# A hybrid decoder trunk on one core: the residual's scale and shift on GpSimd and the router's column sums on VectorE moved to later places, and fourteen instead of two clock-keeping products ahead of the second layer

## The chip, the cores and the metric

The kernel runs on one core of a Trainium2 chip. The metric is the device time of one execution in microseconds. TensorE (PE in the rows) multiplies matrices into PSUM; VectorE (DVE), ScalarE (ACT) and GpSimd (POOL) do the elementwise work; SyncE (SP) issues the transfers. Each engine runs its own instructions strictly in the order of its queue.

## The reference, cut to what matters

Two layers over 256 tokens of width 1024. Each has a token mixer with three branches (latent attention "mla", gated delta rule "dn", HGRN2 "hg"), gated, merged and projected, and then a mixture of experts, each followed by a layer norm of the residual:

```python
h = layer_norm(x, ln_in_g, ln_in_b)
for l in range(DEPTH):
    proj = h @ w_in[l]
    ...
    mixed = (g_a * y_a + g_b * y_b + g_c * y_c) @ w_out[l]
    h = layer_norm(DEEPNORM_ALPHA * h + mixed, ln1_g[l], ln1_b[l])
    moe_out = hier_moe(h, router_group_w[l], router_group_b[l], ...)
    h = layer_norm(DEEPNORM_ALPHA * h + moe_out, ln2_g[l], ln2_b[l])
```

The router inside `hier_moe` multiplies `h` by a 1024 x 36 matrix (4 groups, 32 experts) and adds a bias.

## The kernel before, in words

The input projection's weights come in chunks of up to 1 MB, in a fixed order (`ORDER`), through four buffers. ScalarE rounds a chunk to a high part (L249) and VectorE, for four chunks GpSimd, takes the rest as a low part (L250, "the split"); TensorE adds three products for each pair (L261 to L263, "dense products" here). The branches' small steps lie between dense products on TensorE's queue, so that dense products fill waits as long as there are some ahead of the waiting step.

A layer starts with the norm's statistics on VectorE. A diagonal matrix of the inverse deviations is built from them (tile `sg`, L621), and sixteen products with it turn the residual (L395; each stands in the rows as two). ScalarE and VectorE then write `hTh` and `hTl`, which the dense products read. The norm's true output, which the residual needs only when the mixer's result is added in `project_out`, is made apart: ScalarE scales the tile `res` (L642), GpSimd multiplies it by the norm's weight and adds its bias, 128 x 1024 at a time for two blocks of tokens (L376, L377). The weight and bias lie in two tiles named `o`.

The attention of four heads runs as: query and key products (L1227), query times its rotary table (L1229), scores (L1248), masked maximum on VectorE (L1255), exponentials on ScalarE (L1257), division (L1259, L1261), turning of the weights (L1264) and the product with the values (L1270).

`router_sums` prepares the router's constants. GpSimd multiplies the router's matrix by the norm's weight and bias (L567), VectorE sums over eight slices (L570, 128 x 576 to 128 x 72), adds a bias (L571), TensorE adds over partitions with a matrix of ones, and VectorE copies the result (L574). It is called last in the mixer, but a scheduler sets the order of each engine's queue by what is ready, and `issue_after` puts an instruction behind a named one. So L567 and L570 stood early, at the attention's scores.

Behind the experts of the first layer stands a branch for overflowing experts, which is not taken here. `warm(n)` issues n products of 128 x 128 by 128 x 512 ones in bf16 whose result nobody reads: ten ahead of the branch, two behind it.

Of the kernel before, what the change touches and what calls it, by code (L numbers as in the profile page):

```python
# [15 lines left out]
OP = mybir.AluOpType  # L16
AX = mybir.AxisListType
# [90 lines left out]
class Trunk:  # L108
# [451 lines left out]
        q.dma_start(gb[:, 1], A["ln1_b"][l].rearrange("(p k) -> p k", k=8))  # L560
        self.gb1 = gb[:, 0], gb[:, 1]

    def router_sums(self):

        nc, rw, p = self.nc, self.rw, self.hp
        for i in range(2):
            nc.gpsimd.tensor_tensor(rw[:, :, 36 * i:36 * i + 36], rw[:, :, 36:72],  # L567
                                    self.gbr[i][:, :, None].to_broadcast([128, KT, 36]), op=OP.mult)
        self.rsum = p.tile([128, 72], F32, name="rsum", tag="rsum")
        nc.vector.tensor_reduce(self.rsum, rw.rearrange("p k c -> p c k"), axis=AX.X, op=OP.add)  # L570
        nc.vector.tensor_add(self.rsum[0:1, 36:72], self.rsum[0:1, 36:72], self.rb)  # L571
        ps = self.ps()
        nc.tensor.matmul(ps[:, 0:72], self.ones, self.rsum, start=True, stop=True)
        nc.vector.tensor_copy(self.rsum, ps[:, 0:72])  # L574
# [16 lines left out]
    def layer(self, l):  # L591
        tc, side = self.tc, dict(side="right")
        with ExitStack() as cl, ExitStack() as cr:
            self.ctx_l = cl
            self.sp = cr.enter_context(tc.tile_pool(name=f"split{l}", bufs=1, **side))
            self.gp = cr.enter_context(tc.tile_pool(name=f"merge{l}", bufs=1, **side))
            xp = cr.enter_context(ExitStack())
            hp = xp.enter_context(tc.tile_pool(name=f"x{l}", bufs=1, **side))
            oc = cr.enter_context(ExitStack())
            self.op = oc.enter_context(tc.tile_pool(name=f"o{l}", bufs=1, **side))  # L600
            with tc.tile_pool(name=f"mix{l}", bufs=1) as mp:
                self.mp = mp
                self.open_small(mp, 256)
                if l == 0:
                    rope, src = self.buf("d8", [128, 8, T]), self.A["positions"]
                    self.nc.sync.dma_start(rope[:, 0].bitcast(I32),
                                           bass.AP(tensor=src.tensor, offset=src.offset, ap=[[0, 128], [1, T]]))
                    self.issue(self.wp)
                self.mixer_consts(l, mp)
                if l == 0:  # L610
                    for _ in range(self.NBUF - 2):
                        self.issue(self.wp)
                    self.vrows = self.small_weights(l)
                self.mla_weights(l)
                gb = [x.rearrange("p h t -> p (h t)") for x in self.o4(F32)]
                for x, n in zip(gb, "gb"):
                    self.bcast_row(x, self.A["ln_in_" + n] if l == 0 else self.A["ln2_" + n][l - 1], D)
                self.hT = [hp.tile([128, KT, T], F32R, name=n, tag=n) for n in ("hTh", "hTl")]
                diag = self.gp.tile([128, 4, 128], F32, name="sg", tag="sg", bufs=self.NB["sg"])
                for t in range(TB):  # L620
                    self.nc.vector.tensor_scalar(diag[:, t], self.ident, self.hrs[:, t], None, op0=OP.mult)  # L621
                self.transposed(self.h, self.hT, self.gb0, tmp=lambda: self.buf("d2", [128, 2, T]), scale=diag)
                if l == 0:
                    with tc.issue_after(self.latest(self.nc.tensor)):
                        self.warm(8)
                    with tc.issue_after(self.last_lo.ins):
                        self.rope_tables(rope)
                self.router_weights(l)
                self.mix = self.gp.tile([128, TB, D], F32, name="mix")

                self.pq = self.ps("pm")
                self.chunk_cm(self.pq, l, "cq")
                seq = "dn_decay mla h0 dn_keys dn_inverse dn_queries h1 " \
                      "dn_values hg_forget hg_project hg_local dn_scan hg_scan"
                for n in seq.split():
                    f, a = (self.mla_heads, (int(n[1]),)) if n in ("h0", "h1") else (getattr(self, n), ())
                    self.bank = "pb" if n[:2] == "dn" else "pm"
                    f(l, mp, *a)
                    if f == self.mla:
                        with tc.issue_after(self.last_exp.ins):  # L640
                            for t in range(TB):
                                self.nc.scalar.activation(self.h[:, t], self.h[:, t], AF.Copy, scale=self.hrs[:, t])  # L642
                        with tc.issue_after(self.pool_last.ins):
                            self.scaled(self.h, gb[:1], gb[1:], self.nc.gpsimd)
                        if l == 0:
                            self.nc.gpsimd.tensor_copy(self.bits[:, 1], self.cst("ustrict"))
                        self.dump(f"h2_{l - 1}", self.h.rearrange("p t d -> p (t d)"))
                self.bank = None
                self.merge_branch(l, "a")
                self.gates(l, mp)  # L650
                self.branch_gate(l, mp, "dn", self.dn_o)
                self.branch_gate(l, mp, "hg", self.hg_o)
                self.router_sums()
            self.pw = self.open_prefetch(f"prefetch{l}", self.NPRE)
            self.merge_branch(l, "b")
            def between():

                self.mixS = [hp.tile([128, 8, T], F32R, name=n, tag=n) for n in ("hTh", "hTl")]
                self.mix_turned(0)

            self.merge_branch(l, "c", between)

            oc.close()
            self.open_prefetch(f"more{l}a", 2)

            def free():
                xp.close()
                self.open_prefetch(f"more{l}b", 2)

            self.project_out(l, free)  # L670
            cr.close()
            self.open_prefetch(f"more{l}c", 1)
            with tc.tile_pool(name=f"h1_{l}", bufs=1, **side) as xp, tc.tile_pool(name=f"moe{l}", bufs=1, **side) as ep, \
                    ExitStack() as yc:
                self.moe(l, xp, ep, yc, self.h)
# [5 lines left out]
    def dn_decay(self, l, mp):  # L681
# [57 lines left out]
        nc.vector.tensor_tensor(E, psg.rearrange("p (a i) -> p a i", i=C), c8(gc[:, 0:8]), op=OP.subtract)  # L739
        nc.vector.tensor_tensor(E, E, b8(mincl), op=OP.mult)  # L740
        self.last_exp = nc.scalar.activation(E, E, AF.Exp)
        self.pool_last = nc.gpsimd.tensor_tensor(E, E, b8(mincl), op=OP.mult)
        self.E = E
        ex = self.small([128, 32])
        nc.scalar.activation(ex[:, 0:8], gc[:, 0:8], AF.Exp)
# [378 lines left out]
    def branch_gate(self, l, mp, n, o):  # L1124
        nc = self.nc
        ov = o.rearrange("p t h e -> p (t h) e")
        gv = self.gate[n].rearrange("p t h e -> p (t h) e")
        ss, rs = self.small([128, 8]), self.small([128, 8])
        for i in range(8):
            junk = self.gp.tile([128, 128], F32, name="sg", tag="sg", bufs=self.NB["sg"])  # L1130
            nc.scalar.activation(junk, ov[:, i], AF.Square, accum_out=ss[:, i:i + 1])
        if n == "dn":
            nc.vector.scalar_tensor_tensor(ss, ss, 1.0 / 128, self.dn_eps, op0=OP.mult, op1=OP.add)
        else:
            nc.vector.tensor_scalar(ss, ss, 1.0 / 128, 4 * EPS, op0=OP.mult, op1=OP.add)
        self.rsqrt(rs, ss, self.small([128, 8]))
        for i in range(8):
            nc.vector.scalar_tensor_tensor(ov[:, i], ov[:, i], rs[:, i:i + 1], gv[:, i], op0=OP.mult, op1=OP.mult)
        oT = self.o4()
        for i in range(0, 4, 2):  # L1140
            ps = self.ps()
            for ii in range(2):
                for t in range(TB):
                    nc.tensor.transpose(ps[:, 256 * ii + 128 * t:256 * ii + 128 * t + 128], o[:, t, i + ii], self.ident)
            hi, lo = (x[:, i:i + 2].rearrange("p h t -> p (h t)") for x in oT)
            nc.scalar.activation(hi, ps, AF.Copy, scale=self.on[n])
            nc.vector.scalar_tensor_tensor(lo, ps, self.on[n], hi.bitcast(F32), op0=OP.mult, op1=OP.subtract)
        self.oT[n] = oT
        self.dump_oT(l, n)
# [382 lines left out]
    def moe(self, l, xp, ep, yc, h1):  # L1532
# [200 lines left out]
            self.in_turn(self.warm, 10)  # L1733
        self.overflow(l, ep, rv, past, cmb, xc, total, st)
        if l + 1 < DEPTH:
            self.warm(2)
            self.centred(acc, total, st)
            self.open_banks(f"mix_banks{l}", self.MIX_BANKS, None)
            return
# [53 lines left out]
```

## Time and profile before

| | us |
|---|---|
| median of three runs (1183.57 to 1183.85) | 1183.82 |
| the profiled execution's own time | 1185.7 |
| its span, first instruction to last | 1183.8 |
| TensorE busy in it | 1069.7 (90%) |
| VectorE, ScalarE, GpSimd busy | 593.6, 451.4, 178.7 |
| mean granted clock of TensorE | 0.955 |

A busy share is a mean over stages with different limits. The first layer runs from 0 to about 592 us, the second from there to the end, and each has its mixer first and its experts behind. The granted clock is 1.00 at 2.4 GHz and 0.50 at 1.2 GHz.

### The profile page before, as it was taken

What the parts mean: (1) busy time and instruction counts of PE and PEld (TensorE: products, weight loads), DVE (VectorE), ACT (ScalarE), POOL (GpSimd) and SP (SyncE); (2) the same over time, 40 slices, a digit from 0 to 9 for tenths busy, and PEclk for the clock granted to TensorE, in tenths of its full rate; (3) what the DMA queues carried; (4) which work ended last, traced back from release to release, by engine and by line L of the source; (5) the groups of instructions that cost most, each with busy time, mean ns of one, the idle gap of its engine ahead of it and who ended that gap; (6) DMA issues with size and microseconds to landing.
All of it is one profiled execution on the core that took longest, in us unless ns stands there. A gap on an engine that the chain in (4) does not pass through costs nothing. (4 is left out here: it accounts for less than half of the span.)

```text
span 1183.8 us, 21451 instructions
## 1 busy us (share of the span) xinstructions
PE 1069.7 (90%) x8884; PEld 778.4 (66%) x8884; DVE 593.6 (50%) x1281; ACT 451.4 (38%) x812; POOL 178.7 (15%) x160
## 2 busy tenths in 40 slices
PE   7799998999999999777789999989999999987775
PEld 5688985777777655444377889667777775644442
DVE  7477848466456433111167876574755553321114
ACT  5564553354444222100057545435544442211111
POOL 2410016101120400000024110250012103000001
PEclk9899998999999999888889999989999999988887
DMA  7531341257986799999982314213499669999995
GB/s 231 183 109 37 109 143 37 84 167 292 419 352 225 315 426 425 427 426 427 400 246 74 108 38 143 77 68 126 159 397 424 244 233 417 425 425 426 427 427 207
DMA packets 104706, 305.58 MB, mean 258 GB/s; under 512 B 20962, under 2 KB 48028, under 8 KB 79516
## 3 DMA queue, kind: packets, MB, share of 16 engines
q1 hardware_dynamic: 104604, 304.15, 66.9%
q8 instruction: 72, 1.18, 0.4%
q14 instruction: 30, 0.25, 0.1%
HBM read 303.08 MB, written 1.05 MB: 257 GB/s over the span
## 5 line engine op out<-in xcount | busy, mean ns | idle before, releaser
L250 DVE TENSOR_TENSOR wl<-w,wh 128x1024 fp32r<-128x1024 f32 x150 | 185.6, 1238 | 160.0 <-ACT wh L249 157.3
L249 ACT CAST wh<-w 128x1024 fp32r<-128x1024 f32 x158 | 165.7, 1049 | 199.5 <-PE ps_po L263 68.7
L1620 PE MATMUL ps_pa<-w,xg 128*32 128x256 f32 x2304 | 173.2, 431 | 57.3 <-DMA w<-in_exp_w_up_dram 28.1
L1620 PEld LDWEIGHTS ps_pa<-w,xg 128*32 128x32 f32 x2304 | 84.6, 123 | 140.2 <-DMA w<-in_exp_w_up_dram 37.2
L1632 DVE SCALAR_TENSOR_TENSOR hm<-ps_pa,ws,hm 128x256 f32<-128x256 f32 x18 | 8.7, 484 | 200.7 <-ACT hm L1631 200.5
L1631 ACT ACTIVATE hm<-ps_pa 128x256 f32<-128x256 f32 x18 | 6.9, 385 | 218.7 <-PE ps_pa L1620 218.7
L1653 PE MATMUL ps_pm<-w,hmT 128*32 128x512 f32 x576 | 72.4, 595 | 1.3 <-issue 1.3
L261 PE MATMUL ps_pa<-wh,hTh 128*128 128x512 f32 x176 | 71.4, 405 | 2.0 <-ACT hTh L254 0.7
L261 PE MATMUL ps_po<-wh,hTh 128*128 128x512 f32 x176 | 71.3, 405 | 2.0 <-ACT hTh L254 0.7
L262 PE MATMUL ps_pa<-wl,hTh 128*128 128x512 f32 x176 | 71.1, 404 | 0.9 <-POOL wl L250 0.6
L262 PE MATMUL ps_po<-wl,hTh 128*128 128x512 f32 x176 | 71.0, 404 | 0.9 <-POOL wl L250 0.6
L263 PE MATMUL ps_po<-wh,hTl 128*128 128x512 f32 x176 | 70.9, 403 | 0.2 <-DVE hTl L255 0.2
L263 PE MATMUL ps_pa<-wh,hTl 128*128 128x512 f32 x176 | 70.6, 401 | 0.2 <-DVE hTl L255 0.2
L1570 PEld LDWEIGHTS ps_pm<-P,h1c 128*128 128x128 f32 x576 | 66.8, 192 | 2.2 <-ACT res L1368 1.0
L1570 PE MATMUL ps_pm<-P,h1c 128*128 128x128 f32 x576 | 67.3, 275 | 0.1
L1579 ACT ACTIVATE xg<-ps_pm,gb 128x128 f32<-128x128 f32 x72 | 33.0, 458 | 74.6 <-DVE xg L1577 74.6
L1592 POOL TENSOR_TENSOR Pw<-P,small 128x128 f32<-128x128 f32 x32 | 12.4, 407 | 306.0 <-PE ps_pm L1599 229.5
L1297 POOL TENSOR_TENSOR mix<-mix,sg 128x512 f32<-128x512 f32 x16 | 28.3, 1794 | 153.0 <-DVE sg L1295 153.0
L1577 DVE TENSOR_SCALAR xg<-ps_pm,gb 128x128 f32<-128x128 f32 x72 | 29.4, 408 | 41.1 <-PE ps_pm L1570 32.1
L263 PE MATMUL ps_po<-hTh,wl 128*128 128x256 f32 (+1 forms) x168 | 48.9, 291 | 0.9 <-DVE wl L250 0.5
L261 PE MATMUL ps_pa<-hTh,wh 128*128 128x256 f32 (+1 forms) x168 | 49.5, 295 | 0.0
L263 PE MATMUL ps_pa<-hTh,wl 128*128 128x256 f32 (+1 forms) x168 | 49.0, 292 | 0.5 <-DVE wl L250 0.5
(460 smaller groups left out, 2206.5 us busy)
## 6 DMA issues: line engine op xcount, KB each, us to landing
w<-in_exp_w_gate_dram SPq DMA_DIRECT2D x66, 1024.0 KB
w<-in_exp_w_up_dram SPq DMA_DIRECT2D x66, 1024.0 KB
w<-in_exp_w_down_dram SPq DMA_DIRECT2D x64, 1024.0 KB
w<-in_w_in_dram SPq DMA_DIRECT2D x58, 1024.0 KB
w<-in_w_out_dram SPq DMA_DIRECT2D x8, 1024.0 KB
w<-in_w_br_a_dram SPq DMA_DIRECT2D x4, 1024.0 KB
w<-in_w_br_b_dram SPq DMA_DIRECT2D x4, 1024.0 KB
w<-in_w_br_c_dram SPq DMA_DIRECT2D x4, 1024.0 KB
```

What stands on the lines that cost most here:

```text
L249: nc.scalar.copy(v(hi), raw)
L250: engine.tensor_tensor(v(lo), raw, v(hi).bitcast(F32), op=OP.subtract)
L261: mm(ps, a[0], b[0], start=start, stop=False, skip_group_check=True)
L262: mm(ps, a[0], b[1], start=False, stop=False, skip_group_check=True)
L263: mm(ps, a[1], b[0], start=False, stop=stop, skip_group_check=True)
L1297: nc.gpsimd.tensor_tensor(mv, mv, sg[t], op=OP.add)
L1570: nc.tensor.matmul(ps[:, 128 * k:128 * k + 128], xc[:, t, 4 * h + k], Ps[q][:, t], start=(t == 0), stop=(t == 1))
L1577: nc.vector.tensor_scalar(xg[:, k], o, g, b, op0=OP.mult, op1=OP.add)
L1579: nc.scalar.activation(xg[:, k], o, AF.Identity, scale=g, bias=b)
L1592: self.pool_last = nc.gpsimd.tensor_tensor(e(Pw[:, t]), e(P[:, t]), w, op=OP.mult)
L1620: nc.tensor.matmul(pg[32 * e:32 * e + 32, FF * n:FF * n + FF], xgs[q][k // 4][:, k % 4, 32 * e:32 * e + 32], w[:, FF * k:FF * k + FF], sta ...
L1653: nc.tensor.matmul(ps[c][32 * e:32 * e + 32], hmT[:, i, 32 * e:32 * e + 32], ws[e][:, D * i + 512 * c:D * i + 512 * c + 512], start=(i == ...
```

## The change

Three edits. The four GpSimd instructions that finish the residual are called behind the mixer's scans, and behind whatever stands last on GpSimd's queue there. The router's sum on VectorE is put behind the last instruction of the hg branch's gate (`last_gate`). Behind the overflow branch fourteen clock-keeping products stand instead of two.

```diff
-    def router_sums(self):
+    def router_sums(self, after):
...
-        nc.vector.tensor_reduce(self.rsum, rw.rearrange("p k c -> p c k"), axis=AX.X, op=OP.add)
+        with self.tc.issue_after(after):
+            nc.vector.tensor_reduce(self.rsum, rw.rearrange("p k c -> p c k"), axis=AX.X, op=OP.add)
...
-                        with tc.issue_after(self.pool_last.ins):
-                            self.scaled(self.h, gb[:1], gb[1:], self.nc.gpsimd)
-                        if l == 0:
-                            self.nc.gpsimd.tensor_copy(self.bits[:, 1], self.cst("ustrict"))
...
+                with self.tc.issue_after(self.latest(self.nc.gpsimd)):
+                    self.scaled(self.h, gb[:1], gb[1:], self.nc.gpsimd)
+                    if l == 0:
+                        self.nc.gpsimd.tensor_copy(self.bits[:, 1], self.cst("ustrict"))
...
-                self.router_sums()
+                self.router_sums(self.last_gate.ins)
...
         for i in range(8):
-            nc.vector.scalar_tensor_tensor(ov[:, i], ov[:, i], rs[:, i:i + 1], gv[:, i], op0=OP.mult, op1=OP.mult)
+            self.last_gate = nc.vector.scalar_tensor_tensor(ov[:, i], ov[:, i], rs[:, i:i + 1], gv[:, i], op0=OP.mult,
+                                                            op1=OP.mult)
...
         if l + 1 < DEPTH:
-            self.warm(2)
+            self.warm(14)
             self.centred(acc, total, st)
```

Line numbers of the changed kernel are up to three higher. GpSimd's queue in the first layer, around the residual (`res`), the router's matrix (`rw`) and the delta rule's first tile (`d`), before:

```order
L736 TENSOR_TENSOR d_423<-small,mconst 128x512
L742 TENSOR_TENSOR d_424<-d_424,mconst 128x512
L376 TENSOR_TENSOR res<-res,o_193 128x1024
L377 TENSOR_TENSOR res<-res,o_194 128x1024
L376 TENSOR_TENSOR res<-res,o_193 128x1024
L567 TENSOR_TENSOR rw<-rw,vcols 128x8x36
L377 TENSOR_TENSOR res<-res,o_194 128x1024
L567 TENSOR_TENSOR rw<-rw,vcols 128x8x36
L847 MEMSET d_816 128x1024
```

The same place now:

```order
L738 TENSOR_TENSOR d_423<-small,mconst 128x512
L744 TENSOR_TENSOR d_424<-d_424,mconst 128x512
L567 TENSOR_TENSOR rw<-rw,vcols 128x8x36 x2
L849 MEMSET d_811 128x1024
L875 TENSOR_TENSOR d_809<-d_775,mconst 128x256 x2
```

The four `res` instructions have left it; they stand behind the last GpSimd instruction of the hg scan (L1110 before) and ahead of the next split on GpSimd. VectorE's queue in the second layer, ahead of the attention's scores, before:

```order
L739 TENSOR_TENSOR d_5652<-ps_pb,small 128x512
L255 TENSOR_TENSOR egl<-small,egh 128x8
L570 TENSOR_REDUCE rsum<-rw 128x72
L740 TENSOR_TENSOR d_5652<-d_5652,mconst 128x512
L1197 SCALAR_TENSOR_TENSOR a_5700<-ps_pm,vcols,a_5701 128x256 x2
L1199 SCALAR_TENSOR_TENSOR a_5700<-ps_pm,vcols,a_5701 128x256
L571 TENSOR_TENSOR rsum<-rsum,rb 1x36
L1229 TENSOR_TENSOR a_5733<-ps_pm,qtab 128x512
```

And now:

```order
L741 TENSOR_TENSOR d_5664<-ps_pb,small 128x512
L255 TENSOR_TENSOR egl<-small,egh 128x8
L742 TENSOR_TENSOR d_5664<-d_5664,mconst 128x512
L1200 SCALAR_TENSOR_TENSOR a_5712<-ps_pm,vcols,a_5713 128x256 x2
L1202 SCALAR_TENSOR_TENSOR a_5712<-ps_pm,vcols,a_5713 128x256
L1232 TENSOR_TENSOR a_5741<-ps_pm,qtab 128x512
```

The sum and its bias are gone from there. In the first layer the sum stood directly ahead of the first masked maximum (L1255), and is gone from there too. VectorE's queue in the first layer behind the hg branch's gate (the instruction on `a` x6 is the gate's last six of eight), before:

```order
L1138 SCALAR_TENSOR_TENSOR a_2231<-a_2231,small,a_2588 128x128 x6
L574 COPY rsum<-ps_pb 128x72
L250 TENSOR_TENSOR wl<-w,wh 128x1024
L1147 SCALAR_TENSOR_TENSOR o_2752<-ps_pb,vcols,o_2751 128x512
L1147 SCALAR_TENSOR_TENSOR o_2752<-ps_pm,vcols,o_2751 128x512
```

And now:

```order
L1140 SCALAR_TENSOR_TENSOR a_2226<-a_2226,small,a_2588 128x128 x6
L571 TENSOR_REDUCE rsum<-rw 128x72
L250 TENSOR_TENSOR wl<-w,wh 128x1024
L1150 SCALAR_TENSOR_TENSOR o_2752<-ps_pb,vcols,o_2751 128x512
L1150 SCALAR_TENSOR_TENSOR o_2752<-ps_pm,vcols,o_2751 128x512
L572 TENSOR_TENSOR rsum<-rsum,rb 1x36
```

The sum now stands ahead of a split that TensorE's next dense products read, and the small copy has gone behind the split after it. On ScalarE the second layer's second rounding (L249) now stands ahead of the first step that reads the turned residual instead of behind it. On SyncE, one load of an expert's weights stands ahead of a load of a projection chunk that it followed before.

## Rows read from the trace of the kernel before

**Rows 1.** Waits of TensorE over the span, the longest: us in total, times, longest us.

```profile
PE ps_pa L1620 <- DMA w<-in_exp_w_up_dram: 28.1, 17, 1.9
```

**Rows 2.** Timeline of TensorE, first layer: start us, duration us, instruction, [idle before].

```profile
46.79 0.60 PE L1248 MATMUL ps_pm<-a,a 128*128 128x128 f32 x4
...
56.62 1.08 PE L1264 MATMUL ps_pm<-const,a 128*128 128x128 f32 x4 [7.44 <-DVE a L1261]
...
60.95 0.58 PE L263 MATMUL ps_po<-hTh,wl 128*128 128x256 f32 x1
```

**Rows 3.** Timeline of VectorE, first layer.

```profile
52.87 1.18 DVE L570 TENSOR_REDUCE rsum<-rw 128x72 f32<-128x576 f32 x1 [6.60 <-POOL rw L567]
53.97 0.28 DVE L1255 CUSTOM_DVE_ANT_0 a<-ps_pm,mconst 128x128 f32<-128x128 f32 x1
...
56.19 0.87 DVE L1261 TENSOR_SCALAR a<-a,mla_st 128x128 f32<-128x128 f32 x4
57.53 1.23 DVE L250 TENSOR_TENSOR wl<-w,wh 128x1024 fp32r<-128x1024 f32 x1 [0.47 <-ACT wh L249]
```

**Rows 4.** Timeline of GpSimd, first layer, first of the residual's four.

```profile
42.12 2.37 POOL L376 TENSOR_TENSOR res<-res,o 128x1024 f32<-128x1024 f32 x1 [0.67 <-ACT res L642]
```

**Rows 5.** Busy time by window, first layer; behind the engines: granted clock, DMA share, GB/s.

```profile
55.00:60.00 5.00, 3.34 (x15) 2.41 (x16) 3.51 (x9) 4.73 (x12) 0.00 (x0) 0.50 0.00 0
```

**Rows 6.** Timeline of TensorE, the second layer's start.

```profile
592.00 2.33 PE L365 MATMUL ps_pa<-bits 128*128 128x512 bf16 x10
594.63 0.59 PE L365 MATMUL ps_pa<-bits 128*128 128x512 bf16 x2 [0.30 <-DVE ln_v L333]
598.00 3.76 PE L395 MATMUL ps_pm<-sg,res 128*128 128x128 f32 x16 [2.77 <-DVE sg L621]
601.54 3.08 PE L395 MATMUL ps_pb<-sg,res 128*128 128x128 f32 x16
...
606.79 0.39 PE L262 MATMUL ps_pm<-hTl,wh 128*128 128x256 f32 x1 [1.22 <-DVE hTl L255]
```

**Rows 7.** Busy time by window, the second layer's start.

```profile
598.00:602.00 4.00, 4.00 (x19) 4.00 (x20) 0.75 (x2) 2.70 (x4) 1.19 (x1) 0.50 1.01 239
```

**Rows 8.** Timeline of TensorE, the first layer's start.

```profile
11.09 1.95 PE L395 MATMUL ps_pm<-sg,res 128*128 128x128 f32 x16
```

**Rows 9.** Waits of TensorE from 592 to 640 us.

```profile
PE ps_pm L1264 <- DVE a L1261: 1.7, 1, 1.7
...
PE ps_pm L1203 <- ACT d L741: 0.7, 1, 0.7
```

**Rows 10.** Timeline of VectorE, second layer, around the scores.

```profile
630.59 1.78 DVE L250 TENSOR_TENSOR wl<-w,wh 128x1024 fp32r<-128x1024 f32 x1 [0.39 <-ACT wh L249]
...
636.15 2.34 DVE L1261 TENSOR_SCALAR a<-a,mla_st 128x128 f32<-128x128 f32 x4
```

**Rows 11.** Timeline of VectorE, first layer, behind the gate.

```profile
277.47 0.22 DVE L574 COPY rsum<-ps_pb 128x72 f32<-128x72 f32 x1
277.61 1.21 DVE L250 TENSOR_TENSOR wl<-w,wh 128x1024 fp32r<-128x1024 f32 x1
```

**Rows 12.** Timeline of TensorE, first layer, behind the gate.

```profile
278.88 0.50 PE L262 MATMUL ps_pa<-wl,hTh 128*128 128x512 f32 x1 [0.35 <-DVE wl L250]
```

**Rows 13.** Timelines of GpSimd, VectorE and TensorE, first layer, behind the hg scan.

```profile
214.74 1.05 POOL L1110 TENSOR_TENSOR a<-a,small 128x512 f32<-128x512 f32 x1 [0.80 <-DVE a L1111]
...
223.91 1.23 DVE L250 TENSOR_TENSOR wl<-w,wh 128x1024 fp32r<-128x1024 f32 x1 [5.17 <-ACT wh L249]
...
226.18 0.40 PE L262 MATMUL ps_pa<-wl,o 128*128 128x512 f32 x1
```

**Rows 14.** Busy time by window, ahead of the first layer's experts.

```profile
385.00:395.00 10.00, 10.00 (x157) 7.04 (x155) 5.11 (x35) 3.63 (x10) 0.88 (x2) 1.00 0.35 130
```

**Rows 15.** Timelines of SyncE's queue and ScalarE: a load, and a later rounding of its chunk.

```profile
270.03 8.48 SPq L180 DMA_DIRECT2D w<-in_w_in_dram  x2
...
296.10 1.05 ACT L249 CAST wh<-w 128x1024 fp32r<-128x1024 f32 x1 [2.15 <-PE ps_po L263]
```

More of the change, by code (lines that the diff above doesn't have):

```diff
@@ L642, in layer @@
                                 self.nc.scalar.activation(self.h[:, t], self.h[:, t], AF.Copy, scale=self.hrs[:, t])
-                        with tc.issue_after(self.pool_last.ins):
-                            self.scaled(self.h, gb[:1], gb[1:], self.nc.gpsimd)
-                        if l == 0:
-                            self.nc.gpsimd.tensor_copy(self.bits[:, 1], self.cst("ustrict"))
-                        self.dump(f"h2_{l - 1}", self.h.rearrange("p t d -> p (t d)"))
-                self.bank = None
+                self.bank = None
+                with tc.issue_after(self.latest(self.nc.gpsimd)):
+                    self.scaled(self.h, gb[:1], gb[1:], self.nc.gpsimd)
+                    if l == 0:
+                        self.nc.gpsimd.tensor_copy(self.bits[:, 1], self.cst("ustrict"))
+                self.dump(f"h2_{l - 1}", self.h.rearrange("p t d -> p (t d)"))
                 self.merge_branch(l, "a")
@@ L741, in dn_decay @@
         self.last_exp = nc.scalar.activation(E, E, AF.Exp)
-        self.pool_last = nc.gpsimd.tensor_tensor(E, E, b8(mincl), op=OP.mult)
+        nc.gpsimd.tensor_tensor(E, E, b8(mincl), op=OP.mult)
         self.E = E
```

## The prediction

> **What bounds the kernel now.** I read the page's busy times first (in the table above): TensorE works 90% of the span, so a gain has to come out of its idle time, or out of work that it does at the lower clock. Then its waits, longest first. The longest in total belongs to the experts, where TensorE waits for weights, 28.1 us for one of three kinds, never over 1.9 us at a time [rows 1]; the change doesn't touch that. The longest single waits inside the mixers lie at the edits: ahead of L1264 in the first layer, and ahead of L395 at the second layer's start. The timelines around these two show who is late, and the windows show what clock TensorE had behind them.
>
> In the first layer the scores end at 46.79 + 0.60 = 47.39 [rows 2], but the masked maximum that reads them starts at 53.97 [rows 3]. Ahead of it on VectorE's queue stands the router's sum, which waited 6.60 us for GpSimd's product L567, and GpSimd was busy with the residual's four instructions of 2.37 us from 42.12 [rows 3, 4]. So a sum that only the router needs holds up the attention, and TensorE, out of dense products, stands still for 7.44 us [rows 2]. Behind it the clock is 0.50 [rows 5].
>
> **The change, part by part.** I sum in microseconds; minus is a gain.
>
> *A, the first layer's scores.* With the sum gone, the maximum starts at 47.4 instead of 53.97. From there to L1264 took 56.62 - 53.97 = 2.65 [rows 2, 3]; ScalarE and VectorE lie idle otherwise, and I keep it. L1264 then starts at 50.1, which is 6.5 earlier. TensorE waits under 1 us instead of 7.44 (its dense products ran out at 56.62 - 7.44 = 49.18), and I expect the clock to stay. Before, the stretch from L1264 to the dense product at 60.95, 4.33 us, ran at 0.50 [rows 2, 5]. At full clock its products would take half, but it also holds two trips through ScalarE and VectorE, among them the split that this very product reads, 57.53 + 1.23 = 58.76 [rows 3]. That split comes 6.5 earlier too, so the product could start some 2 us sooner beyond the shift; I take 1.3. A = -6.5 - 1.3 = -7.8, bounds -6.5 (no clock gain) and -8.5.
>
> *B, the second layer's start.* Ten clock-keeping products took 2.33, 0.23 each at 1.00 [rows 6]. Twelve more are 2.8, and the idle time that they fall into is 2.77 [rows 6], so fourteen end about when the diagonal is there: cost 0, at most 0.4. What they buy: TensorE had been idle for 2.77 us, and the thirty-two turning products behind it ran at 0.50 [rows 7], in 3.76 + 3.08 = 6.84 [rows 6]. In the first layer, with busy products right ahead, sixteen of the same took 1.95 [rows 8], so 3.9 for both halves: -2.9. Behind them the dense products then stopped for `hTl` for 1.22 [rows 6]. That chain on VectorE and ScalarE hangs on the turning products and starts earlier; a rounding that stood in the middle of it on ScalarE's queue (about 1 us) now stands ahead of it in idle time. I take 1.0 of the 1.22. B = -3.9, bounds -2.5 and -4.3.
>
> *C, the second layer's scores.* Here GpSimd did its part in time, and the sum ran at once, but directly ahead of the steps that the attention's products needed; TensorE waited 0.7 there. Later it waited 1.7 for the division [rows 9], which took 2.34 instead of 0.87 [rows 3, 10] while GpSimd still worked on the residual. Both causes leave: C = -0.7 - 1.6 = -2.3, bounds -1.7 and -2.6.
>
> *D, the sum at its new place.* It takes 1.18 [rows 3], and the copy of 0.22 that it displaces goes behind the next split. The split behind it ended at 277.61 + 1.21 = 278.82, and TensorE already waited 0.35 for it [rows 11, 12]. So nothing covers the difference: 1.18 - 0.22 = 1.0 us in each layer. D = +2.0, bounds 0 (if TensorE finds products that don't need the split) and 2.8 (if the copy, late now, still costs as much elsewhere).
>
> *E, the residual at its new place.* GpSimd is free from 214.74 + 1.05 = 215.8 [rows 13], and four times 2.37 end at 225.3. Nobody reads the residual until the projection. GpSimd's next instruction is a split for the dn gate, behind the whole merge of the first branch, so I count nothing for its queue. VectorE's work in that stretch is little, but the split at 223.91 falls into it, and TensorE reads its result at 226.18 [rows 13]. The same kind of split met GpSimd at 630.59 and took 1.78 instead of 1.23 [rows 3, 10]; so it would end at 225.7, in time. The most that a row shows, the division's 1.47, gives 226.6, 0.4 late. I take 0, bounds 0 and 0.8 for both layers.
>
> The rows show VectorE slowed beside GpSimd by very different amounts. The Trainium skill, "SBUF — State Buffer", section "SBUF: two separate sides", has a rule for that: the two engines share a pair of ports as an exclusive lock, and whoever comes second waits for the whole instruction of the other. The division agrees with it: it starts at 636.15 and ends only at 638.49. By that rule the split at 223.91 waits for the last of the four to end at 225.3, ends at 226.5, and TensorE loses 0.3 in each layer: the sum would be 0.6 worse.
>
> *Whether the gain reaches the end.* Ahead of the first layer's experts the transfers move at 0.35 of the engines' share [rows 14]: the buffers are full, and loading goes on when TensorE frees them. So the experts' stage, where transfers set the pace, starts earlier by what the mixer gained, and the same holds in the second layer.
>
> Sum: -7.8 - 3.9 - 2.3 + 2.0 + 0 = -12.0. The profiled execution took 1185.7, so 1173.7 for one with a profile. The runs' median, 1183.82, is 1.9 less and equals the span; from it the sum gives **1171.8**.
>
> **The rivals.**
> 1. *The clock is not kept.* If the fourteen don't hold it, or it falls behind the shorter wait of A, what is left is 6.5 + 1.0 + 2.3 - 2.0 = 7.8: 1176.0. Speaking for it: TensorE still waits near 1 us in A, and the clock has fallen after waits. Against: in the first layer's start the same pattern of products kept 1.95 per sixteen [rows 8].
> 2. *The sums cost nothing more and the dense stretch profits in full.* The far ends of A to C and the near end of D: -8.5 - 4.3 - 2.6 + 0 = -15.4, so 1168.4. It needs slack behind the gate, and none shows [rows 12].
> 3. *The transfers take it back.* If loading of experts were the limit from the mixer on, all gains ahead of it would be lost: no change. The share of 0.35 speaks against it [rows 14].
> 4. *Slower: the load that was passed.* On SyncE's queue an expert's load now stands ahead of a projection chunk's load, and it waits for a buffer that the split behind the moved sum frees. Before, the chunk's load was issued at about 278 (270.03 + 8.48), and its rounding started at 296.10, kept by TensorE and not by the transfer [rows 15]. So there are 18 us less one transfer of slack. Each microsecond beyond that stops TensorE in both layers; over 6 us in each eat the 12.0, that is a load that comes some 24 us late. The split is done about 280, which makes that unlikely.
>
> **How the numbers follow.** The forecast with its bounds gets 0.70, rival 1 0.12, rival 2 0.12, rival 3 0.03, rival 4 0.03. The forecast's own bounds, not all at one end, give 1170 to 1175; rivals 1 and 2 widen the range to 1168 to 1177.5. A measurement of this kernel can tell about 0.2%, 2.4 us, from no change. Forecast and rivals 1 and 2 are faster by more, rival 3 is the same, rival 4 slower: 0.94, 0.03, 0.03.
>
> **What would show it.** In the profile after: the masked maximum right behind the scores near 47.4, L1264's counterpart near 50, and a granted clock of 1.00 from 50 to 60 (A). Fourteen products that end near 598 without a fall of the clock, both halves of the turning in about 4 us, and no wait for `hTl` (B). No wait of 0.7 or 1.7 at the second layer's scores (C). TensorE's wait behind the gate grown from 0.35 to about 1.3 in each layer (D). No wait for the split near 226 less the shift (E). The prediction is wrong if the sum behind the gate holds TensorE for longer, if the fourteen products run past the diagonal, or if the experts' stage starts earlier and ends no earlier.

## The result, and the profile after

The changed kernel took 1175.27 us (median of 4 runs, 1172.42 to 1175.78) beside 1183.84 for the kernel before (4 runs): ratio 0.9919, 95% interval 0.9899 to 0.9938. That is faster, by 9.6 us at the ratio, with 7.3 to 12.0 inside the interval (the medians differ by 8.6); the forecast was 12.0 less, at the interval's far end. The profiled execution took 1175.78, its span 1174.0 beside 1183.8. Lines in the changed kernel stand one to three higher than before: L1264 is L1267, L1255 is L1258, L1261 is L1264, L570 is L571.

TensorE's timeline in the first layer, and with it VectorE's and the windows, answer to [rows 2, 3, 5]:

```profile
49.91 0.82 PE L1267 MATMUL ps_pm<-const,a 128*128 128x128 f32 x4 [0.91 <-DVE a L1264]
...
52.79 0.47 PE L263 MATMUL ps_po<-hTh,wl 128*128 128x256 f32 x1
```

```profile
47.25 0.29 DVE L1258 CUSTOM_DVE_ANT_0 a<-ps_pm,mconst 128x128 f32<-128x128 f32 x1 [1.13 <-PE ps_pm L1251]
...
49.48 0.88 DVE L1264 TENSOR_SCALAR a<-a,mla_st 128x128 f32<-128x128 f32 x4
```

```profile
50.00:55.00 5.00, 4.82 (x35) 4.04 (x36) 4.53 (x13) 4.20 (x9) 0.00 (x0) 1.00 0.00 0
55.00:60.00 5.00, 4.94 (x40) 4.27 (x39) 4.43 (x11) 4.24 (x7) 0.00 (x0) 1.00 0.60 180
```

The maximum starts right behind the scores, at 47.25. The wait of 7.44 is 0.91, the clock stays at 1.00, and the dense product at 60.95 starts at 52.79.

TensorE's timeline at the second layer's start, beside [rows 6], and its waits from 587 to 640 us, beside [rows 9] (us in total, times, longest):

```profile
589.65 3.18 PE L365 MATMUL ps_pa<-bits 128*128 128x512 bf16 x14 [0.30 <-DVE ln_v L333]
593.04 2.02 PE L395 MATMUL ps_pm<-sg,res 128*128 128x128 f32 x16 [0.20 <-PE ps_pa L365]
594.90 1.95 PE L395 MATMUL ps_pb<-sg,res 128*128 128x128 f32 x16
```

```profile
PE ps_pa L365 <- DVE ln_v L333: 0.3, 1, 0.3
PE ps_pm L395 <- PE ps_pa L365: 0.2, 1, 0.2
PE ps_pm L1251 <- ACT a L1242: 0.2, 1, 0.2
```

The fourteen products fill the gap to 0.2, both halves of the turning run at a granted clock of 1.00 (593 to 597 us), and the waits for `hTl`, L1203 and L1264 are gone.

Behind the gate it went the other way. VectorE and TensorE there, beside [rows 11, 12]:

```profile
269.34 1.23 DVE L571 TENSOR_REDUCE rsum<-rw 128x72 f32<-128x576 f32 x1
270.48 1.22 DVE L250 TENSOR_TENSOR wl<-w,wh 128x1024 fp32r<-128x1024 f32 x1
```

```profile
271.76 0.50 PE L262 MATMUL ps_pa<-wl,hTh 128*128 128x512 f32 x1 [1.58 <-DVE wl L250]
...
273.50 0.33 PE L574 MATMUL ps_pb<-rsum,ones 128*128 128x72 f32 x2
```

The split starts behind the sum, and TensorE waits 1.58 for it instead of 0.35. The second layer shows the same wait of 1.58, at 848.20. The router's sum over partitions on TensorE (L574, L573 before) now stands behind that wait; before, it ran at 274.10, ahead of it.

GpSimd and VectorE at the residual's new place, beside [rows 13]:

```profile
207.49 4.67 POOL L376 TENSOR_TENSOR res<-res,o 128x1024 f32<-128x1024 f32 x2
212.11 4.72 POOL L377 TENSOR_TENSOR res<-res,o 128x1024 f32<-128x1024 f32 x2
```

```profile
215.65 2.26 DVE L250 TENSOR_TENSOR wl<-w,wh 128x1024 fp32r<-128x1024 f32 x1 [5.18 <-ACT wh L249]
```

GpSimd's last instruction ends at 212.11 + 4.72 = 216.83. The split that starts beside it takes 2.26 instead of 1.23 and ends at 217.91, 1.08 behind GpSimd's end: it got on only when GpSimd was done.

To see where the time went over the whole kernel, I matched TensorE's instructions of both traces in queue order and took the difference of their starts (minus: earlier than before). It changes only in a few places. The first 43 us, which the change hardly touches, differ by -1.4 to +0.5 from the trace before among the twelve others, so a sum over the whole span is known no better than that. The steps, in us, with two more traces of the changed kernel (below):

| stretch (time in the trace before) | term | predicted | changed | again | third |
|---|---|---|---|---|---|
| 0 to 43 | start | 0 | -0.16 | -0.95 | -1.14 |
| 43 to 81 | A | -7.8 | -8.11 | -8.11 | -8.10 |
| 81 to 263 | E, first layer | 0 | +0.12 | +0.20 | +0.16 |
| 263 to 303 | D, first layer | +1.0 | +1.23 | +1.24 | +1.20 |
| 303 to 592 | experts | 0 | +1.93 | +1.44 | +1.34 |
| 592 to 612 | B | -3.9 | -3.97 | -3.99 | -3.97 |
| 612 to 665 | C | -2.3 | -2.09 | -2.09 | -2.09 |
| 665 to 847 | E, second layer | 0 | +0.18 | +0.16 | +0.16 |
| 847 to 880 | D, second layer | +1.0 | +1.20 | +1.21 | +1.23 |
| 880 to the last | experts | 0 | -0.18 | -0.17 | -0.19 |
| sum | | -12.0 | -9.8 | -11.1 | -11.4 |

### The profile page after: what moved, and what is told of

It is laid out like the page before. It is cut to its first block, busy times and chain, and to the rows that moved or that the text cites. A ratio compares the mean times of both kernels' runs of the same rounds, so it can differ in the third digit from the quotient of the medians.

```text
span 1174.0 us, 21469 instructions
## 1 busy us (share of the span) xinstructions
PE 1070.1 (91%) x8896; PEld 776.0 (66%) x8896; DVE 592.7 (50%) x1281; ACT 450.8 (38%) x812; POOL 178.0 (15%) x160
## 5 line engine op out<-in xcount | busy, mean ns | idle before, releaser
L249 ACT CAST wh<-w 128x1024 fp32r<-128x1024 f32 x158 | 165.7, 1049 | 202.5 <-PE ps_pa L263 70.2
L1623 PE MATMUL ps_pa<-w,xg 128*32 128x256 f32 x2304 | 176.7, 437 | 57.2 <-DMA w<-in_exp_w_up_dram 28.3
```

What stands on the lines that cost most here:

```text
L249: nc.scalar.copy(v(hi), raw)
L1623: nc.tensor.matmul(pg[32 * e:32 * e + 32, FF * n:FF * n + FF], xgs[q][k // 4][:, k % 4, 32 * e:32 * e + 32], w[:, FF * k:FF * k + FF], sta ...
```

## The experiments

**The three parts alone.** Each is the kernel before with one part of the change.

```diff
-                        with tc.issue_after(self.pool_last.ins):
-                            self.scaled(self.h, gb[:1], gb[1:], self.nc.gpsimd)
...
+                with tc.issue_after(self.latest(self.nc.gpsimd)):
+                    self.scaled(self.h, gb[:1], gb[1:], self.nc.gpsimd)
```

> Kernel before with only the residual's sum on GpSimd moved behind the mixer's scans. Own theory: in the first layer the router's sum waited only because GpSimd was busy with the residual, so this edit alone frees the masked maximum there and gives the whole of A, -8.1 as the two traces show. In the second layer the division returns to 0.87 us (-1.6), but the sum stays ahead of the attention's steps and the wait of 0.7 stays. No cost D behind the gate, +0.3 for E. Sum -9.4: about 1174.4. Rival: the sum has to leave VectorE's queue for A; then about -1.5, 1182.

Measured: 1175.44 beside 1184.64, ratio 0.9923 (0.9910 to 0.9937), so -9.1. The matched starts give A -8.10, C -1.62, E +0.11 and +0.16, D nothing. VectorE in the first layer:

```profile
42.89 1.19 DVE L570 TENSOR_REDUCE rsum<-rw 128x72 f32<-128x576 f32 x1
...
46.70 0.29 DVE L1256 CUSTOM_DVE_ANT_0 a<-ps_pm,mconst 128x128 f32<-128x128 f32 x1 [1.14 <-PE ps_pm L1249]
```

The sum stands in its old place and holds nobody up: it starts at 42.89, since its product is no longer behind the residual, and the maximum still waits for the scores. A needs this one edit. Of the second layer's two waits, L1264's is gone and that of 0.66 ahead of L1203 has stayed. This trace also has -0.76 in B, with two products as before: TensorE was idle for the same 2.77 and the turning's first half took 3.65, but its second half 1.95 instead of 3.08.

```diff
-        nc.vector.tensor_reduce(self.rsum, rw.rearrange("p k c -> p c k"), axis=AX.X, op=OP.add)
+        with self.tc.issue_after(after):
+            nc.vector.tensor_reduce(self.rsum, rw.rearrange("p k c -> p c k"), axis=AX.X, op=OP.add)
...
-                self.router_sums()
+                self.router_sums(self.last_gate.ins)
```

> Kernel before with only the router's sum on VectorE moved behind the hg gate. Own theory: the maximum no longer stands behind the sum, but GpSimd works on the residual beside the first layer's division, which then takes some 2.3 us as it did in the second layer before; L1264 starts near 51.4 instead of 49.9. First layer -6.6, second -0.7 (the division there stays slow), D +2.4: sum -4.9, about 1179. Rival one, GpSimd beside VectorE costs nothing: -6.4, about 1177.4. Rival two, the longer wait lets the clock fall behind it and only the shift of about 5 is left: -3.3, about 1180.5.

Measured: 1183.78, ratio 0.9993 (0.9984 to 1.0002): no change. All three expectations missed. VectorE, GpSimd and TensorE in the first layer show why:

```profile
46.14 0.29 DVE L1257 CUSTOM_DVE_ANT_0 a<-ps_pm,mconst 128x128 f32<-128x128 f32 x1 [1.14 <-PE ps_pm L1250]
...
48.38 4.24 DVE L1263 TENSOR_SCALAR a<-a,mla_st 128x128 f32<-128x128 f32 x4
```

```profile
45.61 2.40 POOL L376 TENSOR_TENSOR res<-res,o 128x1024 f32<-128x1024 f32 x1
47.96 0.69 POOL L567 TENSOR_TENSOR rw<-rw,vcols 128x288 f32<-128x288 f32 x1
48.59 2.36 POOL L377 TENSOR_TENSOR res<-res,o 128x1024 f32<-128x1024 f32 x1
50.90 0.68 POOL L567 TENSOR_TENSOR rw<-rw,vcols 128x288 f32<-128x288 f32 x1
51.51 0.96 POOL L848 MEMSET d<- 128x1024 f32 x1
```

```profile
48.88 0.30 PE L1266 MATMUL ps_pm<-const,a 128*128 128x128 f32 x1 [0.98 <-DVE a L1263]
51.09 0.33 PE L1266 MATMUL ps_pm<-const,a 128*128 128x128 f32 x1 [1.91 <-DVE a L1263]
52.61 0.69 PE L1266 MATMUL ps_pm<-const,a 128*128 128x128 f32 x2 [1.19 <-DVE a L1263]
```

The maximum is in time, but the division's four instructions of 0.22 take 4.24. TensorE's turnings, which follow them one by one, tell when each was done: the first right behind GpSimd's first L567, the second at about 51, when L377 had ended, the last two at about 52.5, when the shorter ones had. So these divisions get in only where an instruction of GpSimd's ends. The Trainium skill, "SBUF — State Buffer", section "SBUF: two separate sides", has this as an exclusive lock held for a whole instruction, and the trace agrees for these. TensorE stands still three times, its clock from 50 to 55 is 0.71 in the mean, and A is worth -2.20 here. With C -0.98 and D +1.23 and +1.19 only -0.8 is left, which the interval can't tell from nothing.

```diff
-            self.warm(2)
+            self.warm(14)
```

> Kernel before with only fourteen clock-keeping products instead of two. Own theory: B alone, -4.0 at the second layer's first dense products, and all of it reaches the end: about 1179.9. Rival: the products delay the turning and the clock's gain is taken back, about 1184.

Measured: 1180.98, ratio 0.9967 (0.9955 to 0.9979), -3.9. B is -3.97 as in the changed kernel, and it reaches the end.

**The sum's place.** Against the changed kernel:

```diff
+            if c and br == "a":
+                self.router_sums(self.latest(nc.vector))
...
-                self.router_sums(self.last_gate.ins)
```

> Changed kernel with the router's sum put into the first branch's merge, into an idle time of VectorE of 1.59 us ahead of a split that comes every 3 us, instead of behind the hg gate. Own theory: D was the price of the place, so TensorE's wait of 1.58 behind the gate falls back to 0.35 in each layer and nothing new appears: -2.4 against the changed kernel, about 1172.9 (with the changed kernel at 1175.3). Rival: the sum costs wherever it stands, since VectorE's splits are due everywhere: no difference, 1175.3.

Measured: 1171.78, ratio 0.9892 (0.9877 to 0.9907). VectorE in the merge, and TensorE's waits from 225 to 285 us, which hold the place behind the gate as well:

```profile
230.27 1.22 DVE L250 TENSOR_TENSOR wl<-w,wh 128x1024 fp32r<-128x1024 f32 x1 [1.59 <-ACT wh L249]
231.42 1.33 DVE L571 TENSOR_REDUCE rsum<-rw 128x72 f32<-128x576 f32 x1
...
233.08 1.23 DVE L250 TENSOR_TENSOR wl<-w,wh 128x1024 fp32r<-128x1024 f32 x1
```

```profile
PE ps_pa L262 <- POOL wl L250: 0.6, 1, 0.6
PE ps_pa L262 <- DVE wl L250: 0.4, 1, 0.4
PE ps_pa L261 <- DVE mix L1299: 0.3, 1, 0.3
PE ps_pa L261 <- DVE sg L1299: 0.2, 1, 0.2
```

The sum lies in an idle time of VectorE and the wait behind the gate is 0.4 again; one wait of 0.2 in the merge, for `sg`, is new. The matched starts give A, B and C as in the changed kernel. D is -0.14 and -0.16 and E +0.32 and +0.35, since the router's sum over partitions on TensorE has moved from the one stretch into the other; together they are 0.18 and 0.19, beside 0.15 and 0.16 with the residual moved alone. So the sum costs next to nothing here. The time is 1.1 below the expected 1172.9, and that is not the sum's doing: this trace lost only 0.21 in the first layer's experts, where those of the changed kernel lost 1.3 to 1.9. The median is the lowest of all kernels here; a second execution took 1171.80.

The sum back where it stood before, the rest of the change kept:

```diff
-                self.router_sums(self.last_gate.ins)
+                self.router_sums()
```

> Changed kernel with the router's sum undone: residual late and fourteen products, the sum where it stood before. Own theory: D goes (-2.4), the wait of 0.7 at the second layer's scores comes back: -1.7 against the changed kernel, and 0.7 slower than the kernel with the sum in the first merge; ratio to before near 0.990. Rival: the sum has to leave VectorE's queue there, and without it much of A is lost: slower than the changed kernel.

Measured: 1172.1, ratio 0.9894 (0.9879 to 0.9909), beside 1173.98 for the changed kernel, measured together with it, so 1.9 less at the medians, with intervals that overlap. The matched starts say the same: D's 2.4 is gone, and C is -1.64 instead of -2.09. The change without the sum's move is at least as good as the whole; the 0.3 to the kernel with the sum in the first merge is inside the noise. Its profiled execution took 1175.48, over 3 us more than the other three, through a mishap that it shows on VectorE, GpSimd and TensorE:

```profile
587.19 2.18 DVE L338 SCALAR_TENSOR_TENSOR ln_tmp<-ln_tmp 128x2 f32<-128x2 f32 x1
```

```profile
586.99 2.36 POOL L250 TENSOR_TENSOR wl<-w,wh 128x1024 fp32r<-128x1024 f32 x1
```

```profile
592.48 3.42 PE L395 MATMUL ps_pm<-sg,res 128*128 128x128 f32 x16 [2.95 <-issue]
```

One of the norm's small steps, 0.16 in the changed kernel, met GpSimd's split and took 2.18. The diagonal came late, TensorE was idle for 2.95 behind its fourteen products, and the clock, 1.00 at the turning's start, was 0.50 from 593 on: 3.42 instead of 2.02. B is +0.14 in this trace.

**The number of products.** Against the kernel with the sum in the first merge, `self.warm(7)` and `self.warm(24)` in place of `self.warm(14)`.

> Kernel with the sum in the first merge, seven products instead of fourteen: they take 1.6 us, and TensorE then idles some 1.8 us ahead of the diagonal. Theory one, the clock falls behind an idle time of that length: the turning runs at 0.50 again, +4.0, about 1175.8. Theory two, the shorter idle time leaves the clock: no difference, 1171.8.

Measured: 1175.45, ratio 0.9920 (0.9905 to 0.9935). The first theory's number came in, and its mechanism did not. TensorE, then ScalarE, VectorE and GpSimd:

```profile
587.45 1.67 PE L365 MATMUL ps_pa<-bits 128*128 128x512 bf16 x7 [0.30 <-DVE ln_v L333]
590.82 2.02 PE L395 MATMUL ps_pm<-sg,res 128*128 128x128 f32 x16 [1.70 <-ACT res L354]
592.68 1.95 PE L395 MATMUL ps_pb<-sg,res 128*128 128x128 f32 x16
596.07 0.38 PE L262 MATMUL ps_pm<-hTl,wh 128*128 128x256 f32 x1 [1.32 <-DVE hTl L255]
598.38 0.39 PE L262 MATMUL ps_pm<-hTl,wh 128*128 128x256 f32 x1 [1.22 <-DVE hTl L255]
```

```profile
591.54 0.56 ACT L401 ACTIVATE d<-ps_pm,vcol 128x256 f32<-128x256 f32 x1 [1.52 <-PE ps_pm L395]
592.00 1.04 ACT L249 CAST wh<-w 128x1024 fp32r<-128x1024 f32 x1
592.94 0.62 ACT L254 CAST hTh<-d 128x512 fp32r<-128x512 f32 x1
```

```profile
593.79 2.22 DVE L255 TENSOR_TENSOR hTl<-d,hTh 128x512 fp32r<-128x512 f32 x1
597.03 0.24 DVE L499 COPY vcols<-ps_pb 128x77 f32<-128x77 f32 x1 [1.02 <-PE ps_pb L497]
```

```profile
593.12 2.35 POOL L250 TENSOR_TENSOR wl<-w,wh 128x1024 fp32r<-128x1024 f32 x1 [2.59 <-ACT wh L249]
```

The turning took 2.02 and 1.95: the clock was kept with seven products. What came back is two waits for `hTl`, 1.32 and 1.22. The first: with seven, ScalarE's rounding L249 stands between L401 and L254 as in the kernel before; with fourteen it stands ahead of L401. GpSimd's split hangs on that rounding, now falls onto VectorE's L255, and that takes 2.22 instead of 0.69. The second: on VectorE the next L255 stands behind a copy, L499, which waits for a product of TensorE's; so it was in the kernel before, while with fourteen this L255 stands ahead of the copy. The matched starts give B as -1.25 instead of -3.97, so 2.7 of the 4.0 is lost, and none of it to the clock.

> Kernel with the sum in the first merge, twenty-four products instead of fourteen. Ten more at 0.228 us run 2.28 us, of which 0.2 falls into the idle time that is left ahead of the diagonal: +2.1, about 1173.9, if nothing else covers them. Rival: VectorE's and ScalarE's chain behind the turning has slack and the time stays at 1171.8.

Measured: 1173.54, ratio 0.9908 (0.9893 to 0.9924). The products ran 5.34 and the turning started 1.79 later, counted from the first clock-keeping product, than with fourteen; B is -1.98 instead of -3.97, so 2.0 worse, as expected.

**The experts' loss.** The changed kernel was run twice more, unaltered; then with `self.warm(2)` in place of `self.warm(14)`; and the kernel with the sum in the first merge a second time.

> The changed kernel once more, unaltered. Its first trace lost 1.9 us in the first layer's experts: 0.9 where TensorE waited for one gate load of the first expert, 1.0 where the last expert's products ran at a clock of 0.50. Theory one, both are chance: this trace keeps about -7 from the router to the second layer, its span is near 1172. Theory two, both come with the change (other arrival, other order of loads): the same 1.9 is lost again, 1174.

Measured: 1173.98 beside 1184.57, ratio 0.9914 (0.9900 to 0.9928). The wait at the first gate load didn't come again, but 1.44 was lost all the same (table above). So neither theory holds as it was put: the first part of the loss did not come back, the second did.

> Changed kernel with two clock-keeping products as before, residual and sum moved. The products stand behind the first layer's experts, so up to there it should read like the changed kernel. Theory one, the 1.4 to 1.9 us that both traces of the changed kernel lost in the first layer's experts belong to the new places of residual and sum: lost here too. Theory two, they are chance: not lost. Either way B is missing, +4.0 against the changed kernel: about 1178.

Measured: 1177.95, ratio 0.9939 (0.9922 to 0.9955). B is missing, and the experts lost 0.40.

> The changed kernel a third time, for its trace alone. If the loss in the first layer's experts belongs to the kernel, the last expert's up products run at about 6.5 us for 58 again; if it is chance, at 5.2 to 5.4 as in the other kernels.

> The kernel with the sum in the first merge a second time, for its trace alone. If its missing loss there belongs to the kernel, the 58 products take 5.3 us again and the stage loses about 0.2; if it is chance, 6.5 may appear here.

These two took 1174.21 and 1171.80, and lost 1.34 and 0.40 in the first layer's experts. The 58 products of the last expert, first in the kernel before, then in the changed kernel's first trace, with the same products of the expert ahead of it and the window's clock:

```profile
576.83 5.19 PE L1620 MATMUL ps_pa<-w,xg 128*32 128x256 f32 x58 [1.37 <-DMA w<-in_exp_w_up_dram]
```

```profile
541.01 3.64 PE L1623 MATMUL ps_pa<-w,xg 128*32 128x256 f32 x58 [1.85 <-DMA w<-in_exp_w_up_dram]
...
570.57 6.47 PE L1623 MATMUL ps_pa<-w,xg 128*32 128x256 f32 x58 [1.79 <-DMA w<-in_exp_w_up_dram]
```

```profile
569.02:575.02 6.00, 4.45 (x44) 2.11 (x48) 0.00 (x0) 0.00 (x0) 0.00 (x0) 0.54 1.01 427
```

and in the kernel with the sum in the first merge:

```profile
568.16 5.33 PE L1624 MATMUL ps_pa<-w,xg 128*32 128x256 f32 x58 [1.87 <-DMA w<-in_exp_w_up_dram]
```

The third trace of the changed kernel has 6.49 and the one of "again" 6.50. The two traces with the sum in the first merge have 5.33 and 5.46, the kernel with two products 5.38, the kernel before 5.19; all ten traces of other kernels lie between 5.13 and 5.46.

Here TensorE waits for weights again and again, and its clock goes up and down: in the changed kernel's first trace an expert's 58 products take from 3.64 to 6.47. Ahead of the last expert's that costs nothing. The products just before them took 6.27 in the changed kernel, from 560.74, and 3.65 in the kernel before, from 567.00, and in both the 58 started 9.83 after the start of these, when their weights had landed. Only the last ones have no transfer behind them that covers the difference. The second layer's experts vary in the same way with code that no run changed: the kernel with two products lost 0.63 there, that with twenty-four 1.71, the one with the sum in its old place gained 0.50.

## Why the prediction came out as it did

The time lies in the range, and the direction holds, with the mechanisms of A, C and D and half of that of B. The sum was 2.2 us too good against the first trace and the forecast 3.5 against the median: the profiled execution of the kernel before took 1.9 more than its median, that of the changed kernel 0.5 more.

**A** was mis-sized by 0.3: -8.11 for -7.8. L1264 started 6.71 earlier, of which 0.16 stems from the start, so the shift was 6.55 as worked out; the full clock gave 1.45 up to the dense product instead of the 1.3 that I took. One reason was incomplete: I said that the sum holds up the attention. It does, but because GpSimd's product for it stood behind the residual. The residual's move alone gives all of A; the sum's move alone gives -2.20, since the division then runs beside GpSimd.

**B** fits at -3.97, but one of its two terms came in by another way than I gave, which is luck. The 2.9 held: the dense product behind the turning starts 3.56 behind the turning's start instead of 6.38. The 1.0 for `hTl` came to 1.1, yet the wait did not hang on ScalarE's rounding. In the kernel before, VectorE was done with the first L255 at 603.7, when the inputs of the second were there too (the later of them, `hTh` from ScalarE's L254, at 603.44); but the second stood behind the copy L499, which waited for TensorE:

```profile
605.45 0.24 DVE L499 COPY vcols<-ps_pb 128x77 f32<-128x77 f32 x1 [1.74 <-PE ps_pb L497]
```

With fourteen products the order on VectorE has both of these L255 ahead of the copy, and the wait of 1.22 is gone. The run with seven products shows that the two terms are two things. The clock needs fewer products; the rest hangs on the orders on ScalarE and VectorE, which go with their number.

**C** fits at -2.09, from two causes as said: -1.62 with the residual moved alone, -0.98 with the sum moved alone. They overlap by 0.5.

**D** was mis-sized: +1.23 and +1.20 for +1.0 each. The split came later by the 1.0 that I had worked out; the 0.2 that I left out is TensorE's own product for the router (L574), which now stands behind the wait instead of ahead of it. My bound of 0 had no ground, that of 2.8 was near. The sum's move is the one part of the change that costs and gives little: without it, only C's 0.5 would be missing.

**E** was taken as nothing and is +0.12 to +0.20 in each layer. It goes with the residual: the run with the sum moved alone shows 0.00 in both layers. The split ended 1.08 behind GpSimd, as the lock of the Trainium skill ("SBUF — State Buffer", section "SBUF: two separate sides") has it. In size the loss lies midway between the rule's 0.3 in each layer and my 0, since GpSimd's four took 9.34 together instead of 9.5. In mechanism the rule was right and my price was not: the split of 1.78 [rows 10] was no slowed one, it too ended 1.09 behind GpSimd's L377 beside it (last section).

**The step that failed** is the last one, that the experts' stage starts earlier by what the mixer gained and so the gain reaches the end. In the second layer it did. In the first layer's experts 1.93, 1.44 and 1.34 of it were lost in three traces. The transfers took little of it. The first trace's last load of an expert was issued at 563.17 instead of 569.50, so 6.3 earlier, and the last 58 products started 6.26, 7.49 and 7.84 earlier in the three traces, against 6.9, 7.6 and 7.9 at the router: 0.7, 0.1 and 0.0 stayed there. Then these products took 6.47 to 6.50 instead of 5.19, 1.3 more, at a mean clock of 0.55 instead of 0.69 (first trace and kernel before). I had counted nothing for TensorE's clock in that stage. The run with two products is the same kernel up to that point and lost 0.40 in its one trace, so it isn't the new places as such. Why the changed kernel finds the lower clock there in three traces of three stays open.

Of the rivals, the first gave 1176.0 and stands nearer to the median than my 1171.8. It is wrong all the same: the granted clock is 1.00 in both places that it named. The load that was passed (rival 4) did no harm: the rounding at 296.10 [rows 15] starts at 289.18, the shift of 6.9, and is still released by TensorE.

## What to carry to other kernels

When an instruction waits at the head of a queue, look at what it waits for before moving it: here the sum was only the messenger, and moving the work that its producer stood behind gave the gain without moving the sum. Work that may go anywhere belongs into an idle time of its engine, not just behind the last place where it hurt: the same sum cost 1.2 us a layer ahead of a split that was already late and next to nothing 38 us earlier. And match the two traces instruction by instruction: the sum of terms can look right, or a rival's number can come in, with another mechanism behind it.

## What the runs showed of the hardware

- Some instructions of VectorE's beside GpSimd don't slow in proportion, they wait for the end of GpSimd's instruction. Four divisions of 0.22 took 4.24, a step over 128 x 2 elements 2.18 instead of 0.16, a split 2.26 instead of 1.23. Others don't wait: the masked maximum, which reads PSUM, took its 0.29 right beside GpSimd's L376, and the reciprocal ahead of the division its 0.18 beside L567 (48.16).
- It goes both ways: in the kernel before, a split of VectorE that began at 630.59, beside GpSimd's L377, took 1.78, and GpSimd's L376 behind that took 3.37 instead of 2.37:

```profile
628.91 2.37 POOL L377 TENSOR_TENSOR res<-res,o 128x1024 f32<-128x1024 f32 x1
631.23 3.37 POOL L376 TENSOR_TENSOR res<-res,o 128x1024 f32<-128x1024 f32 x1
```

- TensorE's clock behind an idle time at the second layer's start: with 1.70 us idle the turning ran at 1.00; with 2.77 it began at 0.50; with 2.95, behind fourteen products, it began at 1.00 and was at 0.50 from 593 on. That the clock was kept by half of the products I had not expected. The idle time right ahead does not decide it alone: in one trace of the changed kernel 58 products behind a wait of 1.85 took 3.64 at 1.00 and 58 behind a wait of 1.79 took 6.47 at 0.55. Nor is the price fixed: behind 2.77 idle, the turning's second half took 3.08 in the kernel before and 1.95 with the residual moved alone.
